# The branch for tokens beyond the slots, ahead of the last expert pass and inside it

## The chip, the cores and the metric

The kernel runs on one core of a Trainium2 chip. The metric is the device time of one execution in microseconds, the median of several runs; lower is better. An execution has five engines that run side by side: TensorE (PE, with its weight loads PEld), VectorE (DVE), ScalarE (ACT), GpSimd (POOL) and SyncE (SP). SP issues here nearly all transfers from the device's memory, and 16 transfer engines carry them out.

## The reference, cut to what matters

A trunk of two layers over 512 frames of 1024 channels. Each layer is a convolution mixer followed by a mixture of experts, each with a residual sum and a layer normalization. The change lies in the mixture of experts:

```python
def expert_block(args):
    xblk, e = args
    hid = jax.nn.silu(xblk @ w_gate[e]) * (xblk @ w_up[e])
    return hid @ w_down[e]
...
g_idx = jnp.argmax(g_logits, axis=-1)          # one of 4 groups
top_p, top_e = lax.top_k(e_probs, TOP_K)       # 2 of the group's 8 experts
y = jnp.zeros((t, d)).at[sorted_tok].add(contrib)
...
x = layer_norm(ALPHA * x + (1.0 + g_f) * y, ffn_ln_g[i], ffn_ln_b[i])
```

There are 32 experts a layer, each with gate and up (1024 x 512) and down (512 x 1024), all float32, 6 MB an expert. Each of the 512 tokens goes to 2 experts; how many tokens an expert gets is known only when the kernel runs.

## The kernel before, in words

The experts of a layer are worked off in 14 passes (`PASSES`). A pass holds one to four experts that share the 128 columns of TensorE; an expert has 32, 64, 96 or 128 columns there (its slots), and experts with more tokens stand in passes with more slots. The last pass, 13, holds four experts of 32 slots each, so it loads 24 MB and computes little with them. Should an expert have more tokens than slots, the rest is worked off in blocks of 64 by `beyond()`: a branch (`tc.If(most > 0)`) around 32 inner branches and loops. With this kernel's inputs no token lies beyond the slots, so every engine jumps over that code. Each of the five engines runs its own copy of the branch: it loads the count (`TENSOR_LOAD`, L1198), compares, and jumps (`COMPARE_BRANCH`, L1202). On the side that is not taken, each engine brings its semaphores to the counts that they would have on the other side, with waits on line 1202. SP does that for the eight semaphores of the loads: it waits until each has the count of all loads issued so far.

A pass is, in the order of the program: 16 steps `t` of gate and up (L1257), each with one matmul per expert; `combine` (L1139, with the add L1131 on DVE) of the pass before, spread over steps 4, 8 and 12 and the pass's end; `slots_of` at step 12 (L1114 on PE, L1119 to L1127 on DVE), which gives each slot's weight and token; Silu on ACT (L1289), a load of the table for the square root in the last pass (L1291), the product on DVE (L1292), two more combines; the transposition of hid (L1309 on PE, copy L1311 on DVE); down in two halves (L1327), in the last pass with matmuls between them that start the residual sums (L1221); and the scaling (L1339) and splitting (L456, L457) of the result. In layer 0 the next mixer's weights (b_w_in, L141, and ada_w, L124) follow in the same ring of loads.

Loads go through a ring of 6 tiles of 2 MB, each filled by two loads of 1 MB (L174; in the last pass the end of down by loads of 0.5 MB, L184). A tile is loaded again when PE has released it, and SP's queue has eight semaphores, so at most eight loads are in flight. The schedule is written out by hand: what stands earlier in the source stands earlier in every engine's queue. The branch of `beyond()` stands at the start of pass 13, before its first gate matmul. The loads that SP has been given by then, in order, are those up to the second half of pass 13's gate.

Of the kernel before, what the change touches and what calls it, by code (L numbers as in the profile page):

```python
# [45 lines left out]
NP = len(PASSES)  # L46
SLOTS = [n for p in PASSES for n in p]
FIRST = [sum(len(p) for p in PASSES[:g]) for g in range(NP)]
# [14 lines left out]
def trunk_kernel(ctx: ExitStack, tc: tile.TileContext, x, c, ada_w, ada_b, a_w_in, a_b_in, a_w_dw, a_b_dw,  # L63
# [9 lines left out]
    def T(shape, dt, tag, bufs=1):  # L73
        return sb.tile(shape, dt, name=tag, tag=tag, bufs=bufs)
# [239 lines left out]
    for kind in set(PASSES):  # L314
        if len(kind) > 1:
            t = side[kind] = T([128, len(kind)], F32, "side%d" % (len(side),))
# [540 lines left out]
    for i in range(DEPTH):  # L857
# [175 lines left out]
        def by_expert(z):  # L1033
            p = P("a")
            for q in range(NQ):
                PE.transpose(p[:NE, q * 128:(q + 1) * 128], VW[:, z, q, :], ident)
            t = W([NE, 512])
            S.activation(t, p[:NE, :], AF.Copy)
            return t
# [24 lines left out]
        t = by_expert(0)  # L1064
# [68 lines left out]
        def combine(pend, j):  # L1133
            if pend is not None:
                C, ys = pend
                q, d = divmod(j, 2)
                p = P("b")
                for z in range(2):
                    PE.matmul(p, C[:, q * 128:(q + 1) * 128], ys[d][z], start=z == 0, stop=z == 1)  # L1139
                add_out(q, d, p)  # L1140
# [59 lines left out]
        def beyond():  # L1200
            most = blocks(NE)
            with tc.If(most > 0):  # L1202
                tiles = ([W([128, 512], F32R) for _ in range(4)], [W([128, 512]) for _ in range(2)],
                         [W([128, 4, 128]) for _ in range(2)], M([128, 2, 512]))
                for e in range(NE):
                    n = blocks(e)
                    with tc.If(n > 0):
                        eid = bass.ds(nc.values_load(ids[i][:1, e:e + 1], engines=[ET.Activation], min_val=0,
                                                     max_val=NE - 1), 1)
                        V.tensor_scalar(rest, Vd[:, :, e], float(CAP - 32 * SLOTS[e]), None, op0=OP.add)  # L1210
                        with tc.For_i(0, n):
                            V.tensor_scalar(rest, rest, -float(CAP), None, op0=OP.add)
                            block(e, rest, eid, tiles)
# [10 lines left out]
        for g, kind in enumerate(PASSES):  # L1224
            Q, j = g // 2, g % 2
            ns = len(kind)

            wide = kind[0] if len(set(kind)) == 1 else 1
            cols, o = [], 0
            for s, n in enumerate(kind):  # L1230
                for _ in range(n // wide):
                    cols.append((s, 32 * o, 32 * (o + wide)))
                    o += wide
            ohq = lambda q: oh(Q, q, j)
            if g == NP - 1:
                beyond()
            tiles, free = [], 0


            def piece(y):  # L1240
                while len(tiles) <= y // 2:
                    tiles.append(unit())
                return tiles[y // 2][:, y % 2].rearrange("p (k n) -> p k n", k=4)

            def release(y):
                nonlocal free
                while 2 * free + 2 <= y:
                    done()
                    free += 1

            pgu = [P("a"), P("a")]
            for t in range(2 * KD):
                z, k = t // 4 % 2, t // 8 * 4 + t % 4
                if t % 4 == 0:
                    w = [piece(t // 4 * ns + s) for s in range(ns)]
                for s, a, b in cols:
                    PE.matmul(pgu[z][a:b, :], xe(Q, k, j)[:, a:b],  # L1257
                              w[s][:, t % 4, :], start=k == 0,
                              stop=k == KD - 1)
                if t % 4 == 3:  # L1260
                    release((t // 4 + 1) * ns)
                if g == 1:
                    if t == 1:
                        arow, brow = row(pcol("mg", i * 8, 8), ALPHA), row(pcol("mb", i * 8, 8), ALPHA)
                        for q in range(NQ):
                            scale_rows(q, arow, brow)
                    if t in (3, 6):
                        gather(1, 0 if t == 3 else 2)
                    for item in {7: (0,), 9: (1, 2), 11: (3, 4), 13: (5, 6)}.get(t, ()):
                        combine(pend, item)  # L1270
                elif t in (4, 8, 12):
                    combine(pend, t // 2 - 2)
                    combine(pend, t // 2 - 1)
                if g == 0:
                    if t in (1, 4):
                        gather(0, {1: 4, 4: 6}[t])
                    elif t == 6:
                        weigh()
                    elif t == 11:
                        counts()  # L1280
                        ohs.append(pair(1, Vd))
                if i == 0 and g == NP - 1 and t == 1:
                    nxt_aff = affine(pcol("fg", 0, 8), pcol("fb", 0, 8), mod(1, 1), mod(1, 0))
                if i == DEPTH - 1 and g == NP - 1 and t == 13:
                    arow, brow = row(pcol("fg", i * 8, 8)), row(pcol("fb", i * 8, 8))
                if t == 12 and g:
                    ws, C = slots_of(ohq, FIRST[g], kind)
            hid = W([128, 512])
            S.activation(hid, pgu[0], AF.Silu)  # L1289
            if g == NP - 1:  # L1290
                S.activation(warm, epst, AF.Sqrt)  # L1291
            V.tensor_mul(hid, hid, pgu[1])  # L1292
            if g > 1:
                combine(pend, 6)
            combine(pend, 7)

            def ahead(n):
                if 0 < Q < NP // 2 - 1:
                    gather(Q + 1, 4 * j + 2 * n)
                elif g == 1:  # L1300
                    gather(1, 4 + 2 * n)

            if g == 0:
                GF = row(mod(i, 5))
                t = by_expert(1)
            ahead(0)
            pt = P("b")
            for b in range(4):
                PE.transpose(pt[:, b * 128:(b + 1) * 128], hid.rearrange("p (n f) -> p f n", f=4)[:, b], ident)  # L1309
            hT = W([128, 512])  # L1310
            V.tensor_copy(hT, pt)  # L1311
            if g == 0:
                Wd = places(t)
            ahead(1)
            pd = [P("a"), P("a")]
            for u in range(2):
                last = g == NP - 1 and u == 1
                if last:
                    w = [unit(), unit()]
                    w = [[w[d][:, s] for d in range(2)] for s in range(ns)]  # L1320
                else:
                    w = [piece((4 + u) * ns + s) for s in range(ns)]
                    w = [[v.rearrange("p (f d) n -> p f d n", d=2)[:, :, d] for d in range(2)] for v in w]
                for x in range(4):
                    f, d = (x % 2, x // 2) if last else (x // 2, x % 2)
                    for s, a, b in cols:
                        PE.matmul(pd[d][a:b, :], hT[:, (2 * u + f) * 128 + a:(2 * u + f) * 128 + b], w[s][d][:, f, :],  # L1327
                                  start=u + f == 0, stop=u + f == 2)
                    if g == NP - 1 and x % 2 and 2 * u + x // 2 < 2 + i:
                        residual(2 * u + x // 2, ("ba", "bca")[i][2 * u + x // 2])  # L1330
                if last:
                    done(2)
                else:
                    release((5 + u) * ns)
            if g == 0:
                ws, C = slots_of(ohq, FIRST[g], kind)
            ys = [W([128, 512]) for _ in range(2)]
            for d in range(2):
                V.scalar_tensor_tensor(ys[d], pd[d], ws, GF[d], op0=OP.mult, op1=OP.mult)  # L1339
            for d in range(2):  # L1340
                y = W([128, 512], F32R), W([128, 512], F32R)
                split(*y, ys[d])
                ys[d] = y
            pend = (C, ys)
            if j == 1 and Q + 2 < NP // 2:
                ohs.append(pair(Q + 2, Vd))
# [7 lines left out]
        C, ys = pend  # L1354
# [7 lines left out]
        if i == DEPTH - 1:  # L1362
            for n in range(NQ + 1):
# [9 lines left out]
                for h in range(2):  # L1373
                    t = half(q, h)
# [40 lines left out]
        ch, pw, ws = {}, [], []  # L1415
# [49 lines left out]
        for nb in range(KD):  # L1465
            if nb:
                ws = nxt
# [42 lines left out]
            t = W([128, 512])  # L1510
# [35 lines left out]
```

## Time and profile before

| | |
|---|---|
| median of 3 runs | 1492.92 us (1492.81 to 1493.61) |
| the profiled execution | 1491.18 us |
| its span, first to last instruction | 1489.4 us |
| PE busy | 1382.6 us (93%), mean granted clock 0.966 |
| DVE, ACT, POOL busy | 50%, 22%, 18% |
| read from the device's memory | 485.02 MB, 327 GB/s over the span |

All durations in the text come from the one profiled execution. A row of the timeline gives the start and the length in us, engine, line, operation, what is written and read, how many instructions are merged, and in brackets how long the engine was idle before and what ended that. Names of engines with a q (SPq, DVEq) are their instruction queues: branches, waits and issues, which are not counted as busy. [...] A float32 matmul stands in the records twice or more, so counts there are higher than in the program.

### The profile page before, as it was taken

The numbers are of one execution on the slowest core, as the hardware profiler recorded it, in microseconds if no ns is written. First come the engines' busy times: TensorE is split into PE (matmuls) and PEld (weight loads), VectorE is DVE, ScalarE is ACT, GpSimd is POOL, SyncE is SP. The second block draws the span as 40 slices with busy tenths as digits, with TensorE's granted clock in tenths as the row PEclk, the third lists the DMA queues.
The fourth block names the chain that finished last, engine by engine and source line by source line (L and its number), as shares of the span: only waits on it lengthen the run. The fifth ranks groups of instructions, "written<-read, shape, count | busy, mean of one in ns | idle before, by whom it ended". The sixth has DMA issues, their size and how long they took to land. (4 is left out here: it accounts for less than half of the span.)

```text
span 1489.4 us, 20667 instructions
## 1 busy us (share of the span) xinstructions
PE 1382.6 (93%) x8044; PEld 735.5 (49%) x8044; DVE 739.6 (50%) x1426; ACT 325.7 (22%) x547; POOL 263.9 (18%) x275
## 2 busy tenths in 40 slices
PE   4999898999999999997898989999999999999875
PEld 2444477544444444442286767874445444454322
DVE  2799988533343433332267876453334343343215
ACT  1465476210010011000061222422001000011001
POOL 1399942050000000000026051003100000000002
PEclk9999999999999999999999999989999999999988
DMA  8954344799999999999993745239999999999984
GB/s 295 396 213 177 117 154 174 280 420 421 422 419 420 418 421 420 421 421 387 376 279 127 232 173 179 108 147 413 421 421 417 410 416 422 421 421 420 420 356 150
DMA packets 112960, 488.68 MB, mean 328 GB/s; under 512 B 12483, under 2 KB 45771, under 8 KB 63691
## 3 DMA queue, kind: packets, MB, share of 16 engines
q1 hardware_dynamic: 108555, 486.84, 82.1%
q8 instruction: 67, 1.10, 0.3%
q0 software_dynamic: 128, 0.04, 0.2%
q10 hardware_dynamic: 4160, 0.30, 0.2%
q14 instruction: 50, 0.41, 0.1%
HBM read 485.02 MB, written 2.10 MB: 327 GB/s over the span
## 5 line engine op out<-in xcount | busy, mean ns | idle before, releaser
L1257 PE MATMUL pa<-ring,w 128*32 128x512 f32 (+2 forms) x2624 | 438.5, 604 | 26.6 <-DMA ring<-in_e_w_up_dram 15.1
L1131 DVE TENSOR_TENSOR X<-X,pb 128x512 f32<-128x512 f32 x208 | 133.9, 683 | 274.8 <-PE pb L1139 274.8
L1257 PEld LDWEIGHTS pa<-ring,w 128*32 128x32 f32 (+2 forms) x2624 | 120.8, 120 | 274.5 <-issue 227.9
L1327 PE MATMUL pa<-ring,w 128*32 128x512 f32 (+2 forms) x1312 | 209.0, 600 | 9.6 <-DMA ring<-in_e_w_down_dram 6.4
L1139 PE MATMUL pb<-w,w 128*128 128x512 f32 x416 | 130.1, 435 | 0.0
L1327 PEld LDWEIGHTS pa<-ring,w 128*32 128x32 f32 (+2 forms) x1312 | 60.9, 120 | 135.8 <-issue 113.5
L1339 DVE SCALAR_TENSOR_TENSOR w<-pa,ws,w 128x512 f32<-128x512 f32 x56 | 41.9, 750 | 164.9 <-PE pa L1327 162.3
L750 PE MATMUL pa<-RB,ring 128*128 128x512 f32 x256 | 116.5, 612 | 6.2 <-DMA ring<-in_a_w_in_dram 4.2
L1139 PEld LDWEIGHTS pb<-w,w 128*128 128x128 f32 x416 | 72.5, 193 | 97.5 <-issue 80.7
L695 POOL TENSOR_TENSOR w<-w,w 128x512 f32<-128x512 f32 x80 | 104.7, 1309 | 56.2 <-ACT w L693 50.6
L456 ACT ACTIVATE w<-w 128x512 fp32r<-128x512 f32 x58 | 36.6, 630 | 256.8 <-DVE w L1339 256.8
L457 POOL TENSOR_TENSOR RC<-w,RB 128x512 fp32r<-128x512 f32 x8 | 10.9, 1387 | 434.2 <-ACT RB L456 434.2
L1010 ACT ACTIVATE w<-pc,aff 128x256 f32<-128x256 f32 x56 | 31.7, 566 | 253.7 <-PE pc L1005 253.7
L709 DVE SCALAR_TENSOR_TENSOR pb<-RC,w,pb 128x512 f32<-128x512 f32 x126 | 83.6, 745 | 0.0
L750 PEld LDWEIGHTS pa<-RB,ring 128*128 128x128 f32 x256 | 49.1, 196 | 68.8 <-issue 63.3
L1012 DVE TENSOR_SCALAR w<-pc,aff 128x256 f32<-128x256 f32 x56 | 30.5, 544 | 105.8 <-ACT w L1010 105.8
L1289 ACT ACTIVATE w<-pa 128x512 f32<-128x512 f32 x28 | 16.7, 597 | 300.3 <-PE pa L1257 300.3
L1380 POOL TENSOR_TENSOR X<-X,w 128x512 f32<-128x512 f32 x3 | 4.9, 1621 | 426.6 <-ACT X L1379 426.6
L462 PE MATMUL pa<-RB,w 128*128 128x512 f32 x168 | 68.8, 409 | 9.8 <-DVE w L457 9.8
L460 PE MATMUL pa<-RB,w 128*128 128x512 f32 x168 | 68.6, 408 | 0.0
L1005 PE MATMUL pc<-w,RB 128*128 128x256 f32 x448 | 67.1, 295 | 1.5 <-DVE w L977 1.5
L461 PE MATMUL pa<-RC,w 128*128 128x512 f32 x168 | 67.4, 401 | 0.0
(345 smaller groups left out, 1746.1 us busy)
## 6 DMA issues: line engine op xcount, KB each, us to landing
ring<-in_e_w_gate_dram SPq DMA_DIRECT2D x128, 1024.0 KB, 12.6
ring<-in_e_w_up_dram SPq DMA_DIRECT2D x128, 1024.0 KB, 16.1
ring<-in_e_w_down_dram SPq DMA_DIRECT2D x120, 1024.0 KB, 15.8
ring<-in_ada_w_dram SPq DMA_DIRECT2D x14, 2048.0 KB, 11.6
ring<-in_ada_w_dram SPq DMA_DIRECT2D x10, 1536.0 KB, 6.5
ring<-in_b_w_in_dram SPq DMA_DIRECT2D x24, 512.0 KB, 6.5
ring<-in_a_w_in_dram SPq DMA_DIRECT2D x8, 1024.0 KB, 8.2
ring<-in_e_w_down_dram SPq DMA_DIRECT2D x16, 512.0 KB, 13.8
```

Source lines behind the costliest of these rows:

```text
L460: PE.matmul(p, ah, bh, start=start, stop=False)
L461: PE.matmul(p, ah, bl, start=False, stop=False)
L462: PE.matmul(p, al, bh, start=False, stop=stop)
L695: G.tensor_add(vp, vp, z)
L709: V.scalar_tensor_tensor(t if j == TAPS - 1 else acc[n % 2], a, wj, acc[n % 2], op0=OP.mult, op1=OP.add)
L750: PE.matmul(p, w[:, k, h, s], hT[:, k, :], start=k == 0, stop=k == KD - 1)
L1005: PE.matmul(ps[(k - k0) // 2][:, k % 2], src[:, k, q * 128:(q + 1) * 128], oh(Q, q), start=q == 0 and part == 0 and k % 2 == 0, stop=q == ...
L1131: V.tensor_add(half(q, d), half(q, d), p)
L1139: PE.matmul(p, C[:, q * 128:(q + 1) * 128], ys[d][z], start=z == 0, stop=z == 1)
L1257: PE.matmul(pgu[z][a:b, :], xe(Q, k, j)[:, a:b], w[s][:, t % 4, :], start=k == 0, stop=k == KD - 1)
L1327: PE.matmul(pd[d][a:b, :], hT[:, (2 * u + f) * 128 + a:(2 * u + f) * 128 + b], w[s][d][:, f, :], start=u + f == 0, stop=u + f == 2)
L1339: V.scalar_tensor_tensor(ys[d], pd[d], ws, GF[d], op0=OP.mult, op1=OP.mult)
```

## The change

The call of `beyond()` moves from the start of pass 13 to behind the last combine of that pass, between gate and up and the transposition of hid. In this pass `slots_of` moves from step 12 to just behind the branch.

```diff
@@ -1232,8 +1232,6 @@
             ohq = lambda q: oh(Q, q, j)
-            if g == NP - 1:
-                beyond()
             tiles, free = [], 0
@@ -1283,7 +1281,7 @@
-                if t == 12 and g:
+                if t == 12 and 0 < g < NP - 1:
                     ws, C = slots_of(ohq, FIRST[g], kind)
             hid = W([128, 512])
             S.activation(hid, pgu[0], AF.Silu)
@@ -1293,6 +1291,10 @@
             if g > 1:
                 combine(pend, 6)
             combine(pend, 7)
+
+            if g == NP - 1:
+                beyond()
+                ws, C = slots_of(ohq, FIRST[g], kind)
 
             def ahead(n):
```

Lines from L1237 on have a number lower by 2 in the changed kernel up to L1296, and higher by 2 behind it (L1309 is L1311 there, L1311 is L1313, L1327 is L1329).

SP, layer 0, the instructions up to the branch. Before, the branch follows the last load of gate:

```order
L174 ISA
L174 DMA ring<-in_e_w_gate_dram 128x2048
L1198 TENSOR_LOAD nbi
L1198 ISA x2
L1202 COMPARE_AND_BRANCH
```

In the changed kernel it follows the loads of up and down (L174, L184) and six of the next mixer:

```order
L184 ISA
L184 DMA ring<-in_e_w_down_dram 128x2x512
L141 DMA ring<-in_b_w_in_dram 128x8x128 x6
L1198 TENSOR_LOAD nbi
L1198 ISA x2
L1202 COMPARE_AND_BRANCH
```

So 16 loads of the pass and 6 of b_w_in are now ahead of SP's branch. In layer 1 the 16 loads are the kernel's last.

DVE, layer 0, in pass 13 (X is the residual sum, ws the weights of the slots, the numbered tiles hid, the matrix of tokens and the transposed hid). Before, all of it stands behind the branch:

```order
L1131 TENSOR_TENSOR X<-X,pb 128x512 x6
L1119 SCALAR_TENSOR_TENSOR ws<-pc,side_213 128x8
L1123 COPY ws<-pc 128x1
L1127 TENSOR_SCALAR w_10964<-slot,ws 128x128 x4
L1292 TENSOR_TENSOR w_10989<-w_10989,pa 128x512
L1131 TENSOR_TENSOR X<-X,pb 128x512 x2
L1311 COPY w_11006<-pb 128x512
```

In the changed kernel the branch follows the last two adds:

```order
L1131 TENSOR_TENSOR X<-X,pb 128x512 x6
L1290 TENSOR_TENSOR w_5224<-w_5224,pa 128x512
L1131 TENSOR_TENSOR X<-X,pb 128x512 x2
L1198 TENSOR_LOAD nbi
L1202 COMPARE_AND_BRANCH
```

and behind it stand, on the side that is not taken:

```order
L1119 SCALAR_TENSOR_TENSOR ws<-pc,side_213 128x8
L1123 COPY ws<-pc 128x1
L1127 TENSOR_SCALAR w_10996<-slot,ws 128x128 x4
L1313 COPY w_11006<-pb 128x512
L1341 SCALAR_TENSOR_TENSOR w_11063<-pa,ws,w_2277 128x512
```

The jump and the three lines of slots_of now stand between the last add and the copy of the transposed hid.

ACT, layer 0, from the last pass's Silu to the first normalization (mv holds mean and variance, few a constant). Before:

```order
L1289 ACTIVATE w_10989<-pa 128x512
L1291 ACT_TABLE_LOAD
L1291 ACTIVATE few<-few 128x1
L456 ACTIVATE w_11067<-w_11063 128x512
L456 ACTIVATE w_11071<-w_11064 128x512
L475 ACTIVATE mv<-mv,few 128x1
```

In the changed kernel, behind the branch:

```order
L456 ACT_TABLE_LOAD
L456 ACTIVATE w_11067<-w_11063 128x512
L456 ACTIVATE w_11071<-w_11064 128x512
L475 ACT_TABLE_LOAD
L475 ACTIVATE mv<-mv,few 128x1
```

The load of L1291 (L1289 in the changed kernel) stays ahead of the branch, and two more table loads stand behind it.

## Rows read from the trace of the kernel before

**Rows 1.** Stretches of 5 us: busy by engine, PEclk, DMA share, GB/s.
```profile
685.00:690.00 5.00, 3.98 (x22) 1.81 (x26) 0.59 (x1) 0.00 (x0) 0.00 (x0) 0.66 1.03 418
...
705.00:710.00 5.00, 3.59 (x16) 1.10 (x18) 1.21 (x2) 0.00 (x0) 0.00 (x0) 1.00 0.38 111
...
715.00:720.00 5.00, 2.96 (x4) 0.32 (x4) 0.00 (x0) 0.00 (x0) 0.00 (x0) 0.71 1.02 433
720.00:725.00 5.00, 4.90 (x18) 2.41 (x22) 1.59 (x6) 0.00 (x0) 0.00 (x0) 0.61 1.01 424
...
1425.00:1430.00 5.00, 3.08 (x5) 0.51 (x6) 0.00 (x0) 0.00 (x0) 0.00 (x0) 0.70 0.21 57
```

**Rows 2.** Timeline of SP's issues around layer 0's last pass.
```profile
680.01 7.17 SPq L174 DMA_DIRECT2D ring<-in_e_w_gate_dram  x4
707.49 2.16 SPq L174 DMA_DIRECT2D ring<-in_e_w_up_dram  x4
...
759.95 8.74 SPq L141 DMA_DIRECT2D ring<-in_b_w_in_dram  x3
...
777.18 0.37 SPq L124 DMA_DIRECT2D ring<-in_ada_w_dram  x1
```

**Rows 3.** Lines 1198 and 1202, layer 0: ns min/median/max, first and last start.
```profile
L1198 DVEq TENSOR_LOAD <-nbi x1: 542/542/542, 684.9 to 684.9; - x1
L1198 PEldq TENSOR_LOAD <-nbi x1: 491/491/491, 679.0 to 679.0; - x1
...
L1202 SPq EVENT_SEMAPHORE  x9: 17/17/17, 693.2 to 707.2; - x9
```

**Rows 4.** Timeline around layer 0's branch.
```profile
684.12 1.47 DVE L457 TENSOR_TENSOR w<-w,w 128x512 fp32r<-128x512 f32 x2
...
686.02 6.89 PE L1257 MATMUL pa<-ring,w 128*32 128x512 f32 x36 [2.62 <-PEq L1202]
...
691.35 0.17 DVE L438 TENSOR_TENSOR affA<-colP,mods 128x8 f32<-128x8 f32 x1 [5.77 <-DVEq L1202]
```

**Rows 5.** Timeline, layer 0, from the end of gate to down.
```profile
707.03 1.04 PE L1257 MATMUL pa<-ring,w 128*32 128x512 f32 x2 [1.41 <-SPq L1202]
...
717.62 1.91 PE L1257 MATMUL pa<-ring,w 128*32 128x512 f32 x2 [1.44 <-DMA ring<-in_e_w_up_dram]
...
720.10 1.91 PE L1257 MATMUL pa<-ring,w 128*32 128x512 f32 x2 [0.57 <-DMA ring<-in_e_w_up_dram]
...
723.82 0.55 PE L1114 MATMUL pc<-w,w 128*128 128x16 f32 x4
...
724.66 0.16 DVE L1119 SCALAR_TENSOR_TENSOR ws<-pc,side 128x8 f32<-128x8 f32 x1
...
724.93 0.88 DVE L1127 TENSOR_SCALAR w<-slot,ws 128x128 fp32r<-128x128 f32 x4
...
727.85 1.28 DVE L1131 TENSOR_TENSOR X<-X,pb 128x512 f32<-128x512 f32 x2
...
729.37 0.69 DVE L1311 COPY w<-pb 128x512 f32<-128x512 f32 x1 [0.24 <-PE pb L1309]
...
730.12 1.92 PE L1327 MATMUL pa<-ring,w 128*32 128x512 f32 x16 [0.78 <-DVE w L1311]
...
737.65 2.77 PE L1327 MATMUL pa<-ring,w 128*32 128x512 f32 x20
...
742.11 1.90 PE L1327 MATMUL pa<-ring,w 128*32 128x512 f32 x10 [0.34 <-DMA ring<-in_e_w_down_dram]
```

**Rows 6.** The same in layer 1: the last load before SP's issues resume, the last up part.
```profile
1427.96 1.92 PE L1257 MATMUL pa<-ring,w 128*32 128x512 f32 x2 [1.41 <-SPq L1202]
...
1441.63 1.92 PE L1257 MATMUL pa<-ring,w 128*32 128x512 f32 x2 [1.44 <-DMA ring<-in_e_w_up_dram]
```

**Rows 7.** Timeline of ACT, layer 0, the table load and the first normalization.
```profile
712.64 1.28 ACT L1291 ACT_TABLE_LOAD   x1
...
747.82 0.29 ACT L475 ACTIVATE mv<-mv,few 128x1 f32<-128x1 f32 x1 [2.29 <-DVE mv L472]
```

## The prediction

> **What bounds the kernel now.** I read the page first, then the bandwidth by stretches of 5 us around the two last expert passes (pass 13 of each layer), then the queue of SP, which issues every weight load, then the branch's own lines, and last the timeline of the end of each last pass.
>
> The stretches show that the expert passes run at the rate of the weight loads: 433 and 424 GB/s behind 715 us, with PE starved (2.96 us busy of 5) [rows 1]. Once in each layer the rate falls, to 111 GB/s at 705 us and 57 GB/s at 1425 us [rows 1]. SP's queue says why: its last issue before the branch ends at 687.2 us and the next one starts at 707.49 [rows 2]. In between stand nine waits of line 1202, from 693.2 to 707.2 us [rows 3]: where the branch is not taken, SP waits until every load in flight has landed. The transfer engines drain and start again.
>
> The other engines pay for the branch too. DVE loads the branch's value at 684.9 us, as the second of its two L457 starts, and its next operation is at 691.35 with 5.77 us idle: 6.45 us from load to operation [rows 3, 4]. PE loads it at 679.0, while matmuls are still queued, so only 2.62 us of its jump show [rows 3, 4]. Here both lie where PE soon waits for loads anyway: they cost nothing now, and only SP's drain reaches the end.
>
> **The change part by part.**
>
> *SP's drain goes.* Landings can be read from PE, which starts as each of the last parts arrives: 707.03 for the last load before the drain, 717.62 and 720.10 for the last two up parts, 2.48 us apart [rows 5]. Without a gap the fourth landing after 707.03 comes 4 x 2.48 = 9.92 us later; it takes 13.07. Layer 0 gains 3.15 us. In layer 1, 1427.96 to 1441.63 is 13.67 us: a gain of 3.75 [rows 6]. Counted in bytes from the two empty stretches alone it is more, (420-111) x 5/420 = 3.7 and (420-57) x 5/420 = 4.3 us [rows 1]; I take the landings, since PE waits for the last part of a load, and keep the bytes as the other end (1.1 us more gain in all).
>
> *SP's branch at its new place.* Ahead of it now stand all loads of the pass and, in layer 0, six of b_w_in. Behind it wait the next loads of ada_w and b_w_in. Before, SP had issued three b_w_in loads by 768.7 us and then stood until 777.18 for a free slot [rows 2]: 8.5 us of cover. The jump and drain delay the issues behind them by less than that, so I cost it at nothing; without the cover it would be some 5 us. In layer 1 only the output follows.
>
> *PE's branch.* Its start-of-pass gap of 2.62 us [rows 4] goes, but PE then waited for loads, so nothing is gained. At the new place PE runs ahead as before; there it was 4.4 us ahead (686.02 - 2.62 - 679.0), here I take 3 us, an estimate, since the matmuls it has queued are shorter. It needs 7.0 us from load to matmul [rows 3, 4], and so is through about 4 us after its last combine, before DVE is.
>
> *DVE's branch, the term that decides.* Before, the second L1131 add of the pass starts at about 728.45 (two in 1.28 us from 727.85) and the first down matmul at 730.12: 1.67 us, through the copy of the transposed hid at 729.37 [rows 5]. Now the branch stands behind that add. The add waits for PE's last combine, so DVE's queue cannot be past it earlier; the load of the value starts with the add, as it did with the second L457. Then 6.45 us to the first operation [rows 4]; the four lines of slots_of, now ahead of the copy, 724.66 to 725.81 = 1.15 us; copy to first down matmul 0.75 us [rows 5]. That is 8.35 us instead of 1.67: +6.7. PE no longer does slots_of's matmuls ahead of the last gate and up, -0.5 (0.55 in its row [rows 5]). Net **+6.2 us** a layer between the last landing and the first down matmul. Bounds: if DVE showed only what PE showed of its branch, 2.62 us in place of 6.45 [rows 4], +2.4; upward I see no row beyond +6.7.
>
> [...]
>
> *The down stage.* Layer 0: start shift 6.2 - 3.15 = +3.05. Before, the last part of down was waited for: its second half started at 737.65 and after 16 matmul records (1.92 us) wanted a part that came at 742.11 [rows 5], a stall of 2.5 us. Now that part lands at about 738.96 and is wanted at 742.6: the stall is gone. The end of down moves by 3.05 - 2.5 = **+0.55**. Layer 1: 6.2 - 3.75 = **+2.45**, and no load was late there. At full clock the sum is +3.0 us.
>
> *PE's clock.* The new wait leaves PE nearly idle from its last combine (before 728.45) to the down matmuls 8.3 us later, with only slots_of and the transpositions (about 1.2 us) inside. [...] I take **2.5 us** a layer, 5.0 in all. [...]
>
> *ACT's tables.* The branch now stands behind the load of the table for the square root, so ACT loads again ahead of L456 and of L475, 1.28 us each [rows 7]. ACT sat idle for 2.29 us ahead of L475 [rows 7]: hidden, with 1 us to spare. In layer 1 the load ahead of L456 stands behind a wait, but what decides is the second half of down, 16 matmul records and more behind it. If the cover failed, +1.3 us a layer.
>
> Sum: 0.55 + 2.45 + 5.0 = **+8.0 us** on the profiled execution's 1491.18 (span 1489.4 and 1.8 around it): 1499.2. The median of the runs, 1492.92, stands 1.74 above that execution, so the time I name is **1500.9**.
>
> **The rivals.**
>
> *A: the clock holds.* [...] For it: a granted clock is not lost after every short wait. [...] Time: 1492.92 + 3.0 = 1495.9, or 1494.8 if the gap also gives back its bytes.
>
> *B: the jump is short at the new place.* If DVE and PE find the code behind the branch at hand, DVE pays the load of 0.54 us [rows 3] and next to nothing more: -3.15 + 0.6 + 1.15 - 0.5 = -1.9 at the start of down in layer 0, its end held to -3.15 by the landing; -2.5 in layer 1, no spell of low clock: -5.65, or 1487.3. It decides at the first DVE operation behind the branch. Against it: the same body of code is jumped over, and both engines showed 6.5 to 7 us from load to operation [rows 3, 4]. [...]
>
> *C: more is exposed.* ACT's table loads fall on the path, or a spell of low clock lasts through down: up to 2 x (1.3 + 0.9) = 4.4 more, 1505.
>
> **How the numbers follow.** Forecast 0.65, A 0.19, B 0.06, C 0.10. About 0.2% (3 us) is what a measurement of this kernel can tell from no change. Forecast and C are slower, B is faster; of A, which lies on the line, I count 0.13 as no change and 0.06 as slower. So slower 0.81, same 0.13, faster 0.06. The range reaches down into A and up to C: 1494.5 to 1505; the forecast's own, with 1.7 to 3.4 us of clock a layer and the shifting spells, is 1497 to 1504.
>
> **What would show it.** Right: no stretch under 350 GB/s between 690 and 725 us; SP's nine waits behind the last loads; DVE idle for about 5.8 us on its own branch directly ahead of L1119; the first down matmul about 8 us after PE's last combine; a granted clock under 0.8 there; no wait for a load inside down in layer 0. Wrong: DVE's operations follow the branch within 1 us, or down starts earlier after the last landing than 13 us, or the drop in bandwidth stays.

## The result, and the profile after

The changed kernel takes 1499.55 us (median of 5 runs, 1498.84 to 1501.2) beside 1492.81 for the kernel before on the same chip: by the medians it is 6.7 us slower. The ratio of the runs is 1.0061 (95% interval 1.0044 to 1.0078), which would be 9.1 us (6.6 to 11.6); the medians lie at the lower end of that. Forecast were 8.0 us slower, 1500.9.

The stretches of the changed kernel around its two last passes, with the columns of [rows 1]:

```profile
705.00:710.00 5.00, 3.60 (x21) 1.15 (x18) 0.57 (x1) 0.00 (x0) 0.00 (x0) 1.00 1.01 421
...
725.00:730.00 5.00, 0.13 (x1) 0.00 (x0) 1.05 (x2) 0.00 (x0) 0.00 (x0) 0.77 1.03 386
730.00:735.00 5.00, 2.43 (x12) 1.80 (x16) 1.72 (x8) 0.00 (x0) 0.00 (x0) 0.50 1.05 385
735.00:740.00 5.00, 5.00 (x24) 1.12 (x20) 0.00 (x0) 0.00 (x0) 0.00 (x0) 0.71 1.05 310
...
745.00:750.00 5.00, 3.90 (x29) 1.34 (x22) 3.23 (x5) 2.40 (x3) 0.00 (x0) 1.00 0.50 126
```

The drop to 111 GB/s at 705 us [rows 1] is gone. In its place PE is busy for 0.13 us of the five behind 725, and its granted clock is down to 0.50 when it starts again. The loads pause once, at 745 us, where b_w_in was ahead of its need.

Lines 1202 and 1198 of the changed kernel (ns min/median/max, then the first start, in layer 0, and the last, in layer 1; compare [rows 3]):

```profile
L1202 SPq EVENT_SEMAPHORE  x18: 17/17/17, 748.1 to 1462.8; - x18
...
L1202 PEldq EVENT_SEMAPHORE  x4: 51/51/51, 728.8 to 1455.7; - x4
L1202 DVEq EVENT_SEMAPHORE  x4: 21/21/21, 731.5 to 1457.3; - x4
...
L1202 PEldq COMPARE_BRANCH  x2: 6081/6190/6299, 722.7 to 1449.2; - x2
L1202 DVEq COMPARE_BRANCH  x2: 72/72/72, 725.8 to 1451.5; - x2
```

```profile
L1198 PEldq TENSOR_LOAD <-nbi x2: 315/402/489, 722.1 to 1448.7; - x2
L1198 DVEq TENSOR_LOAD <-nbi x2: 331/436/541, 725.2 to 1451.1; - x2
```

SP's waits now stand behind the pass's loads (748.1 us). PE reads the branch's value 3.1 us ahead of DVE (722.1 and 725.2) and is behind its branch at 728.8, DVE at 731.5. The timeline of layer 0 shows what that does (compare [rows 5]):

```profile
717.65 1.92 PE L1255 MATMUL pa<-ring,w 128*32 128x512 f32 x2 [1.46 <-DMA ring<-in_e_w_up_dram]
718.82 1.28 ACT L456 ACT_TABLE_LOAD   x1 [3.99 <-ACTq L1202]
...
724.77 1.28 DVE L1131 TENSOR_TENSOR X<-X,pb 128x512 f32<-128x512 f32 x2
...
731.70 0.99 PE L1114 MATMUL pc<-w,w 128*128 128x16 f32 x4 [6.58 <-DVEq L1202]
...
732.73 0.17 DVE L1119 SCALAR_TENSOR_TENSOR ws<-pc,side 128x8 f32<-128x8 f32 x1 [6.68 <-PE pc L1114]
...
734.54 3.56 PE L1329 MATMUL pa<-ring,w 128*32 128x512 f32 x16 [0.86 <-DVE w L1313]
...
739.95 1.92 PE L1329 MATMUL pa<-ring,w 128*32 128x512 f32 x16
...
743.72 3.64 PE L1329 MATMUL pa<-ring,w 128*32 128x512 f32 x32
...
751.13 0.29 ACT L475 ACTIVATE mv<-mv,few 128x1 f32<-128x1 f32 x1 [0.99 <-DVE mv L472]
```

Read it from the end of down: its 32 matmul records at 743.72 no longer wait for a load (compare 742.11 in [rows 5]); its first 16 take 3.56 us where a later 16 take 1.92, which is the low clock (0.53 granted from 734.5 to 738.1 us, 1.00 from 738 to 744); and ahead of them DVE and PE stand still for 6.6 us.

To add the terms up, marks of the kernel before that were not shown yet. L1339 is the scaling of down's result; the first of each pair belongs to pass 12, the second is the last of pass 13:

```profile
682.59 1.61 DVE L1339 SCALAR_TENSOR_TENSOR w<-pa,ws,w 128x512 f32<-128x512 f32 x2 [6.33 <-PE pa L1327]
...
744.05 0.75 DVE L1339 SCALAR_TENSOR_TENSOR w<-pa,ws,w 128x512 f32<-128x512 f32 x1 [3.66 <-PE pa L1327]
...
1403.81 1.61 DVE L1339 SCALAR_TENSOR_TENSOR w<-pa,ws,w 128x512 f32<-128x512 f32 x2 [6.33 <-PE pa L1327]
...
1452.86 1.28 DVE L1131 TENSOR_TENSOR X<-X,pb 128x512 f32<-128x512 f32 x2
...
1455.13 1.92 PE L1327 MATMUL pa<-ring,w 128*32 128x512 f32 x16 [0.79 <-DVE w L1311]
...
1468.42 0.75 DVE L1339 SCALAR_TENSOR_TENSOR w<-pa,ws,w 128x512 f32<-128x512 f32 x1 [3.02 <-PE pa L1327]
```

The same of the changed kernel (the scaling is L1341 there):

```profile
683.45 1.61 DVE L1341 SCALAR_TENSOR_TENSOR w<-pa,ws,w 128x512 f32<-128x512 f32 x2 [6.33 <-PE pa L1329]
...
747.43 0.75 DVE L1341 SCALAR_TENSOR_TENSOR w<-pa,ws,w 128x512 f32<-128x512 f32 x1 [0.97 <-PE pa L1329]
...
1407.11 1.61 DVE L1341 SCALAR_TENSOR_TENSOR w<-pa,ws,w 128x512 f32<-128x512 f32 x2 [6.33 <-PE pa L1329]
...
1440.84 1.75 PE L1255 MATMUL pa<-ring,w 128*32 128x512 f32 x2 [1.44 <-DMA ring<-in_e_w_up_dram]
...
1450.65 1.28 DVE L1131 TENSOR_TENSOR X<-X,pb 128x512 f32<-128x512 f32 x2
...
1460.16 3.64 PE L1329 MATMUL pa<-ring,w 128*32 128x512 f32 x16 [0.87 <-DVE w L1313]
...
1475.76 0.75 DVE L1341 SCALAR_TENSOR_TENSOR w<-pa,ws,w 128x512 f32<-128x512 f32 x1 [3.02 <-PE pa L1329]
```

The stages between these marks, in us, with the second add taken 0.64 us behind the start of its pair:

| stage of pass 13 | layer 0: before, after, difference | layer 1 |
|---|---|---|
| scaling of pass 12 to the last up part | 37.51, 34.20, **-3.31** | 37.82, 33.73, **-4.09** |
| last up part to the second of the last adds | 8.39, 7.76, **-0.63** | 11.87, 10.45, **-1.42** |
| that add to the first down matmul | 1.63, 9.13, **+7.50** | 1.63, 8.87, **+7.24** |
| down, to the last scaling | 13.93, 12.89, **-1.04** | 13.29, 15.60, **+2.31** |
| sum | **+2.52** | **+4.04** |

With -0.08 us in the mixer between the layers (1403.81 - 744.05 = 659.76, 1407.11 - 747.43 = 659.68) that is 6.5 us, about what the medians say. Each column is one execution. In the other runs with the branch at its old place in a layer, with the long body or a short one, the two scalings of layer 0 lie 61.16 and 61.82 us apart (61.46 here), those of layer 1 62.35 and 65.72 (64.61 here); with the change in that layer alone it is 64.16 and 68.83 (63.98 and 68.65 here). So the +2.52 of layer 0 is firm to about half a us, the +4.04 of layer 1 to about two. The two profiled spans differ by more, 8.3 us (1489.4 and 1497.7): 0.86 of it stands at 682.59 and 683.45 already, ahead of the change, and 0.9 behind the last operations, in the output's transfers.

### The profile page after: what moved, and what is told of

Its sections match the earlier page's. It is cut to its first block, busy times and chain, and to the rows that moved or that the text cites. A ratio compares the mean times of both kernels' runs of the same rounds, so it can differ in the third digit from the quotient of the medians.

```text
span 1497.7 us, 20663 instructions
## 1 busy us (share of the span) xinstructions
PE 1384.9 (92%) x8044; PEld 734.6 (49%) x8044; DVE 739.4 (49%) x1426; ACT 330.8 (22%) x551; POOL 263.7 (18%) x275
## 5 line engine op out<-in xcount | busy, mean ns | idle before, releaser
L1329 PE MATMUL pa<-ring,w 128*32 128x512 f32 (+2 forms) x1312 | 211.1, 615 | 9.1 <-DMA ring<-in_e_w_down_dram 5.8
L1329 PEld LDWEIGHTS pa<-ring,w 128*32 128x32 f32 (+2 forms) x1312 | 61.1, 122 | 136.1 <-issue 115.3
L1341 DVE SCALAR_TENSOR_TENSOR w<-pa,ws,w 128x512 f32<-128x512 f32 x56 | 41.9, 751 | 167.0 <-PE pa L1329 164.4
L456 ACT ACTIVATE w<-w 128x512 fp32r<-128x512 f32 x58 | 36.6, 630 | 241.2 <-DVE w L1341 241.2
```

## The experiments

Differences from the kernel before are given by the ratio of the runs on the same chip; by that measure the changed kernel is 9.1 us slower. The theory: at its old place the branch cost SP's drain of the loads alone; at the new one it costs the jumps of DVE and PE, which nothing hides. The rivals: the drain was hidden anyway; the moved slots_of is what costs; a jump costs the same anywhere in the pass.

**No branch.** Edit, on the kernel before:

```diff
-            if g == NP - 1:
-                beyond()
```

> The kernel before without the call of beyond() in either layer (it leaves out the work for tokens beyond the slots, of which these inputs have none); all else as before. Theory: at its old place the branch cost what its drain of the loads cost, 3.3 us in layer 0 and 4.1 us in layer 1 between the end of pass 12 and the landing of the last up part; so the time is 1492.8 - 7.4 = 1485.4 us, no stretch below 350 GB/s inside pass 13. Rival 1, the drain was taken up by other waits and cost nothing: 1492.8. Rival 2, it also cost clock and jumps on PE and DVE: below 1483.

Measured: 0.9950 (0.9934 to 0.9965), 7.5 us less than before. The drain cost what the landings said, and rival 1 is out. In its trace the stretch between the two scalings is 56.88 and 59.86 us in place of 61.46 and 64.61: 4.6 and 4.75 less, somewhat over the landings' part: up to the last up part it is 34.11 and 34.14 us, 3.40 and 3.68 less.

**slots_of ahead of the branch.** Edit, on the changed kernel (its weights in a tile of their own):

```diff
-                if t == 12 and 0 < g < NP - 1:
+                if t == 12 and g:
...
                 beyond()
-                ws, C = slots_of(ohq, FIRST[g], kind)
```

> The changed kernel with slots_of of the last pass back at step 12, ahead of the branch (its weights in a tile of their own), and only the branch between the last combine and the transposition. Theory, that the jump decides: DVE is through the branch at the same time, the transposition and its copy follow at once, so down starts 1.0 us earlier after the jump, while slots_of's matmuls come back ahead of the last add (0.6 us in layer 0, 1.4 in layer 1): 1499.5 within 1.5 us. Rival, that moving slots_of behind the branch is what costs: at least half of the 6.7 us comes back, 1496 or below.

Measured: 1.0049 (1.0035 to 1.0064), 7.3 us over the kernel before, within the noise of the changed kernel and far from the half that the rival wants back. In the trace 1.0 us a layer comes back where the theory has it: from the second add to down it is 8.11 and 7.81 us, not 9.13 and 8.87. The rest is the jump's, not slots_of's.

**The branch at step 12.** Edit, on the kernel before:

```diff
-            if g == NP - 1:
-                beyond()
...
                     w = [piece(t // 4 * ns + s) for s in range(ns)]
+                if g == NP - 1 and t == 12:
+                    beyond()
```

> The kernel before with the branch moved to step 12 of pass 13, ahead of that step's matmuls and with slots_of behind it as before. Theory: all loads of the pass are issued by then, so SP's waits delay none of them (-3.3 and -4.1 us as in the kernel without branch), and the jumps of PE and DVE lie in the wait for the last four up parts (PE idle or starved from 710 to 717.6 us in the changed kernel): 1485.4 to 1488 us. Rival 1, a jump is paid wherever it stands inside the pass: 6 to 7 us a layer on top, 1498. Rival 2, SP's waits now stand ahead of all of b_w_in and the next mixer waits for it: 1488 to 1492, with the loss in layer 0 alone.

Measured: 1481.92 us beside 1490.67, 0.9945 (0.9925 to 0.9965), 8.2 us less than before: as good as no branch, faster than both kernels, and somewhat better than the theory's 4.8 to 7.4 us less. Its timeline, layer 0:

```profile
711.14 15.82 SPq L184 DMA_DIRECT2D ring<-in_e_w_down_dram  x8
...
715.56 2.66 PE L1257 MATMUL pa<-ring,w 128*32 128x512 f32 x8 [4.44 <-PEq L1202]
...
726.17 2.00 PE L1327 MATMUL pa<-ring,w 128*32 128x512 f32 x16 [0.78 <-DVE w L1311]
```

PE is idle for 4.44 us on its own branch, where it would have waited for the last up parts; the last half loads of down are issued regardless; down starts at a granted clock of 1.00 (725 to 730 us). Rival 2 is not borne out: b_w_in starts at 737 us and the mixer takes 1.8 us longer than before (661.57 beside 659.76 between the scalings, 659.99 without a branch), but among all the runs it takes between 657.81 (all waits filled) and 662.02 us (short body), so 1.8 us of one execution shows nothing.

**The branch behind the copy.** Edit, on the kernel before, with slots_of's weights in a tile of their own:

```diff
             V.tensor_copy(hT, pt)
+            if g == NP - 1:
+                beyond()
```

> The branch one step later than in the changed kernel: behind the transposition and its copy on DVE, ahead of the first down matmul; slots_of at step 12 as before. So DVE's jump lies beside the down matmuls and only PE's own jump can stand ahead of down. Theory: both engines jump about 6.2 us; PE's begins while its last matmuls are queued (3 us ahead in the changed kernel), so down starts 3 to 4 us after the copy, 4 to 5 us less per layer than in the changed kernel: 1490 to 1494 us with its spells of low clock. Rival 1, DVE's jump alone was the cost and PE hides its own: 1486 to 1488. Rival 2, the first down matmul waits for DVE's semaphores behind the branch as slots_of did: 1499.

Measured: 1.0044 (1.0029 to 1.0059), 6.6 us over the kernel before: the theory's 1490 to 1494 is missed. Rival 2's size came, and its mechanism with it, though PE's own jump would have done nearly the same. The trace:

```profile
726.99 0.75 PE L1307 MATMUL pb<-ident,w 128*128 128x128 f32 x4 [0.38 <-DVE X L1131]
...
734.26 0.23 PEld L1327 LDWEIGHTS pa<-ring,w 128*32 128x32 f32 x8 [6.72 <-DVEq L1202]
...
1460.19 3.64 PE L1327 MATMUL pa<-ring,w 128*32 128x512 f32 x16 [6.39 <-DVEq L1202]
```

```profile
L1202 PEldq EVENT_SEMAPHORE  x4: 51/51/51, 733.9 to 1459.9; - x4
...
L1202 DVEq EVENT_SEMAPHORE  x4: 21/21/21, 734.1 to 1460.2; - x4
```

```profile
L1198 PEldq TENSOR_LOAD <-nbi x2: 319/404/490, 727.0 to 1453.1; - x2
```

PE loads the branch's value at 727.0, with the start of the transposition, not 3 us ahead of it: the transposition waits for DVE's adds (they free its bank), and PE's queue, and with it the branch, waits behind it. So PE is behind its own branch only at 733.9, 6.9 us after that load. What ended the wait of down's weights is, by the profile, DVE's line 1202 (6.72 us; in layer 1 too): DVE writes the transposed hid that down reads, and brings up its count behind its branch, at 734.1. DVE's branch is last by some 0.2 us, so without it PE's would have held down almost as long. The run does not separate the two prices; it shows that both jumps end together here and that neither is hidden.

**One layer alone.** The change with a condition on the layer, `if i == 0` or `if i == 1`, the other layer as before.

> The change in layer 0 alone; layer 1 has the branch at the start of its last pass, as before. Theory, by the marks in the traces of before and changed (second L1341 of pass 13 less the L1341 of pass 12): +2.5 us on the kernel before, with the drain of layer 1 back at 57 GB/s. Rival, that SP's new stand ahead of the next mixer's weights is what costs: +6 us or more, all of the loss in this layer.

> The change in layer 1 alone. Theory, by the same marks: +4.0 us on the kernel before (no load of down was late there, so the whole shift reaches the end). With the run for layer 0 the sum is the changed kernel's +6.7. Rival, as for layer 0 alone: 0 to 1 us.

Measured: 1.0021 (1.0010 to 1.0031) and 1.0030 (1.0016 to 1.0044), that is 3.1 and 4.5 us. Each is slower by itself. The loss in layer 1, behind which no mixer stands, and at most 4.6 us in layer 0 exclude the mixer's weights as the cause; that layer 1 loses more is what the stages of the table say, but the two intervals overlap.

**PE kept busy.** Edit, on the changed kernel, ahead of the branch:

```diff
+                pd = [P("a"), P("a")]
+                for _ in range(6):
+                    PE.matmul(pd[0], ident, GF[0], start=True, stop=True)
                 beyond()
```

> The changed kernel with six matmuls of 128x512 float32 (about 1 us each, the identity on a constant, into the bank that down will overwrite) between the last combine and the branch on PE. [...] Rival 1, the slow start of down is not the clock of an idle PE: +6.7 as the changed kernel. Rival 2, the six matmuls hold back PE's own jump until it ends behind DVE's: +7 or more, with down at full clock.

Measured: 1.0046 (1.0031 to 1.0062), 6.9 us over the kernel before. The author's estimate was +2.5, with down's first 16 matmuls in 1.92 us: missed. Layer 0:

```profile
733.27 0.58 PE L1114 MATMUL pc<-w,w 128*128 128x16 f32 x4 [1.39 <-DVEq L1202]
...
735.70 3.11 PE L1333 MATMUL pa<-ring,w 128*32 128x512 f32 x16 [1.24 <-DVE w L1316]
```

slots_of's matmuls now run at a granted clock of 1.00 (732.5 to 735 us; 0.58 us, not 0.99), but behind the waits of 1.39 and 1.24 us the clock falls in down (0.76 and 0.56 in the two stretches of 2.5 us behind 735): the price moved. In layer 1 it did not fall, behind waits of 1.14 and 1.24 us:

```profile
1460.00:1465.00 5.00, 3.01 (x21) 0.80 (x20) 1.65 (x8) 0.00 (x0) 0.00 (x0) 1.00 0.33 124
```

Down takes 14.64 us there and not 15.60, although PE stands 0.75 us in it with no wait that the profile shows. But between the last add and down it is still 8.68 and 8.45 us: the wait for the jumps stays, and it is most of the loss.

**All waits of PE filled.** The run before with a seventh matmul, and one more behind the transposition.

> The run with PE kept busy, with a seventh such matmul ahead of the branch and one more between the transposition and down, so that no wait of PE between the last combine and down is over about 0.6 us (1.39 and 1.24 us with six). Theory, that the clock falls with such short waits too: down's first 16 matmuls take 1.92 us and not 3.1 to 3.6, the two residual matmuls 1.98 and not 2.5, so 1.5 us a layer less than with six: +3 to +4 us on the kernel before. Rival, the clock falls at that place whatever PE does (a fixed time after the starved part of the pass): 16 matmuls again over 3 us, +6 to +7.

Measured: 1.0074 (1.0051 to 1.0096), 11 us over the kernel before: the time is missed by far, and only the clock of layer 0 behaved. First a stretch of layer 0, then the timeline of both layers:

```profile
735.00:740.00 5.00, 4.57 (x23) 1.36 (x26) 0.00 (x0) 0.00 (x0) 0.00 (x0) 1.00 0.94 295
```

```profile
735.43 1.91 PE L1335 MATMUL pa<-ring,w 128*32 128x512 f32 x11 [1.32 <-issue]
...
1458.35 2.08 PE L1316 MATMUL pa<-w,ident 128*128 128x512 f32 x2 [3.49 <-issue]
```

In layer 0 the granted clock stays at 1.00 through down, where the changed kernel had 0.71 (735 to 740 us). But PE now stands 3.49 us in layer 1, and 1.32 us inside down in layer 0, with nothing that the profile shows to wait for. In the idle stretch of layer 1, 1454.9 to 1458.35 us, three packets ran on the queues for instructions; what PE waited for there is not shown. So the low clock can be avoided (layer 0 here, layer 1 in the run before), which excludes the rival that it falls there whatever PE does; but the time was not had back.

**A short body.** Edit, on the changed kernel: `for e in range(1)` in place of `range(NE)` inside beyond().

> The changed kernel with one expert in place of 32 inside beyond() (it leaves out the work beyond the slots for experts 1 to 31, of which these inputs have none), so that DVE jumps over 21 instructions and not 672. Theory, that the jump's time is the fetch of code that isn't at hand: if 21 instructions lie in what has been fetched, the 5.6 us from DVE's branch to its next instruction fall below 1 us on all engines, and the time falls to about 1483 + 2 = 1485 to 1488. Rival, the jump's time doesn't depend on its length: DVE 5.6 us and PE 6.2 us as before, +6.7.

Measured: 0.9976 (0.9961 to 0.9990), 3.6 us less than before and 10 or more less than the changed kernel. That is just over the expected 1488 (1488.26 us), and less of a gain than the 5 to 8 us that the expectation meant. Line 1202 of it, and the start of down in layer 0:

```profile
L1202 DVEq EVENT_SEMAPHORE  x4: 21/21/21, 728.6 to 1451.1; - x4
...
L1202 PEldq COMPARE_BRANCH  x2: 365/366/367, 724.8 to 1448.1; - x2
L1202 DVEq COMPARE_BRANCH  x2: 72/74/76, 728.0 to 1450.8; - x2
```

```profile
731.14 3.64 PE L1329 MATMUL pa<-ring,w 128*32 128x512 f32 x16 [1.24 <-DVE w L1313]
```

DVE needs 0.6 us from its branch to the code behind it in place of 5.7, PE's branch takes 0.37 us and not 6.2. So the jump's time depends here on what is jumped over: one expert's code, or that of 32. (The 21 and 672 of the expectation leave out the register, semaphore and branch instructions in that code.) The slow start of down stays (3.64 us for its first 16 records, 1.93 for a later 16) after a wait that is much shorter. Beside the run without a branch, 7.5 us less than before, some 4 us are left: from the second add to down it is still 3.58 and 3.39 us, not 1.63, and down starts slowly in both layers (3.64 and 3.52 us).

**A short body at the old place.** The same edit on the kernel before.

> The kernel before, branch at the start of the last pass, with one expert in place of 32 inside beyond() (it leaves out the work beyond the slots for experts 1 to 31, of which these inputs have none). In the changed place the short body cut DVE's jump from 5.7 to 0.6 us. Theory: at the old place the jumps lie in the wait for loads and only SP's waits for the loads in flight cost, so nothing changes: within 1.5 us of the kernel before, the drop in bandwidth stays. Rival, SP's own jump or that of PE and DVE was part of the old place's cost: 3 to 7 us less than before.

Measured: 1.0004 (0.9992 to 1.0017), no change. The jumps are shorter here too (DVE idle for 0.75 us, not 5.77; PE's branch 0.36 us in one layer and 2.87 in the other), the drop stays:

```profile
705.00:710.00 5.00, 3.44 (x12) 1.10 (x16) 0.65 (x2) 0.00 (x0) 0.00 (x0) 1.00 0.29 90
```

```profile
687.14 0.17 DVE L438 TENSOR_TENSOR affA<-colP,mods 128x8 f32<-128x8 f32 x1 [0.75 <-DVEq L1202]
```

So at the old place the drain costs and the jumps do not. At the new one the drain is gone and the jumps over the long body are most of the price; the rest, some 4 us, stays with the short body too.

**The branch at step 8.** As at step 12, with `t == 8`.

> The branch at step 8 of pass 13 in place of step 12, else as in the run with step 12. PE and DVE are starved there too, so their jumps stay hidden; but at step 8 the last 8 half loads of down (4 MB) are not yet issued, and stand behind SP's waits. Theory: the loads then restart once more, 2 us or so after the last one in flight has landed, so the end of down comes 1.5 to 3 us later a layer than with step 12: 3 to 6 us above that run, 3 to 6 below the kernel before. Rival 1, the place of SP's branch among the loads doesn't matter as long as the jumps are hidden: as step 12, 8 to 9 us below the kernel before. Rival 2, the drain costs its full 3.3 and 4.1 us here as well: same as before.

Measured: 0.9975 (0.9961 to 0.9989), 3.7 us less than before, 4.5 more than at step 12, as the theory had it. The half loads that were issued from 711.14 us at step 12 now wait for the drain:

```profile
730.12 6.16 SPq L184 DMA_DIRECT2D ring<-in_e_w_down_dram  x8
```

## Why the prediction was right, point by point

- **SP's drain goes:** right. Forecast -3.15 and -3.75 us, measured -3.31 and -4.09; the run without a branch shows it by itself (-3.40 and -3.68). By the bytes of the empty stretches it would have been 3.7 and 4.3; the table's values lie between.
- **SP's branch at its new place costs nothing:** not contradicted. The mixer took 0.08 us less, though the loads pause (126 GB/s at 745 us); but its time scatters by some 2 us among the runs, so less than that could not be seen.
- **PE's branch is through before DVE's:** right (728.8 and 731.5 us; it began 3.0 us ahead of the end of the last combine, as taken). What the sum made of it was wrong: it has the first of slots_of's lines on DVE follow DVE's branch at once, as if PE had done slots_of's matmuls by then. These matmuls (L1114) waited 6.58 us, by the profile for DVE's line 1202: their bank is freed by DVE, whose count is brought up only behind its branch. That put them, and 1.2 us from 731.5 to 732.73, on the path.
- **DVE's branch, the term that decides:** right in kind, short in size: forecast +6.7 from add to down, measured +7.50 and +7.24, by the step just named. The bound that PE's row gave (+2.4) was far off: 2.62 us showed there only because PE had run ahead.
- **-0.5 us for slots_of gone from the last gate and up:** right for layer 0 (-0.63, of which 0.47 is L1114). In layer 1 it is -1.42: 0.79 for L1114, which ran at the low clock before (0.50 granted from 1444 to 1446 us), and 0.65 because the eight records of L1257 behind it took 1.72 us before and 1.07 after, the clock again (0.62 from 1446 to 1448 us before, 1.00 from 1444.6 to 1446.2 after). That part is luck of the two executions: in the other runs with the branch at its old place in that layer this stage took 9.14 and 10.50 us in layer 0 (8.39 here) and 9.62 and 11.79 in layer 1 (11.87 here).
- **The stall in down goes (layer 0), nothing is late in layer 1:** right. The part of down behind its first half took 10.17 us before (733.88 to 744.05) and 7.48 after (739.95 to 747.43), so the stall was 2.7 us, forecast 2.5.
- **The clock, 2.5 us a layer:** right in kind, somewhat too large in layer 0. The 2.5 us, and the 1.7 to 3.4 and the shifting spells of the range, were the author's estimate, and no run shows them as such. What the runs showed in their place: the first half of down took 5.41 us and not 3.76 in layer 0 (+1.65), 6.07 and not 3.77 in layer 1 (+2.30). In the kernel before, stretches of 0.5 us from 685 to 700 us have a granted clock of 1.00 or 0.50, and a value between (0.84, 0.74, 0.58) only where it changes; read so, the 0.66, 0.71 and 0.61 of [rows 1] are 3.4, 2.9 and 3.9 us at 0.50. The granted clock fell as forecast (under 0.8; 0.50 from 730 to 735 us and from 1460.2 to 1463.8), and rival A, that it holds, is out; it had held, at 1.00 from 730 to 732 us, behind the 0.78 us wait ahead of down in the kernel before [rows 5]. Down started as slowly (3.64 us for 16) after the 3.6 us from add to down of the short body, and the clock held in down where PE was given other work: in layer 0 with all waits filled (1.00 from 735 to 745 us), in layer 1 with six matmuls (1.00 from 1460 to 1465), with which it still fell in layer 0 (0.66 from 735 to 740).
- **ACT's tables cost nothing:** right; the load ahead of L456 came at 718.82 us, long before its use, and L475 had its table 0.99 us before DVE gave it its input. In layer 1 the load stood ahead of the first L456 (1472.82 us), and the second still waited 1.86 us for DVE. So this half of rival C is out, and so is the other: down's later matmuls ran at 1.92 us for 16.
- **Rival B, a short jump:** excluded by the result (5.7 and 6.2 us), but the short body shows that it was a question of the body's length: with one expert's code in place of 32 the jump is as short as the rival has it (0.6 us on DVE, 0.37 on PE). That the time is a fetch of code is not shown.

The sum, 8.0 forecast and 6.5 by the stages, is off by down (-1.2, of which the clock is -1.05), slots_of's share (-1.05) and the drain (-0.5), against +1.3 for the wait behind DVE's branch. That these errors partly cancel is luck; the terms that decide, the drain, the wait on DVE's branch and the clock, were each forecast by their mechanism and lay within 1 us a layer.

## What to carry to other kernels

Here the branch that is not taken had two prices, and they fell on different engines: SP, whose queue issues the loads, waited for all of them (3.31 and 4.09 us more up to the last up part at the old place), and the others stood still while they jumped over the code (5.6 to 6.3 us over the long body). Put it where the loads ahead of it are all issued and the computing engines wait for data anyway (here step 12 of the pass, 8.2 us less than before); only one of the two is half the job. In these traces an engine read its branch's value only when what stands before it had been sent off (behind the copy PE read it at 727.0 us, with the start of the transposition), so count its lead from its last wait, not from its last instruction. And what one engine frees for another it may hand over only behind its own branch: here PE, through at 728.8 us, stood until DVE was through at 731.5.

## What the runs showed of the hardware

The jump's time goes with the code jumped over: in the run of the change PE's branch took 6.1 and 6.3 us over the long body, and 0.37 in both layers over the short one; with the short body at the old place it took 0.36 us in one layer and 2.87 in the other. Only these two lengths were measured. The instruction queues (packets, MB, share) go with it, though they do not show whose code they carry; from 722 to 745 us, first the changed kernel, then the one with the short body:

```profile
q8 instruction: 3, 0.05, 0.9%
q14 instruction: 3, 0.02, 0.3%
```

```profile
q8 instruction: 1, 0.02, 0.3%
q14 instruction: 1, 0.01, 0.1%
```

And in these two runs the slow start of down did not follow the length of the wait: down's first 16 matmuls took 3.56 us where 9.1 us lay between the last add and down, and 3.64 us where 3.6 lay between them.
